# Streaming-encoder layer: more buffers in the first stage, and the recurrence's chained small products spread over more steps

## The chip, the cores and the metric

The kernel runs on one core of one Trainium2 chip. The metric is the device time of one execution in microseconds (us), as the median of three runs. A core has a matrix engine (TensorE, PE in the profile), a vector engine (VectorE, DVE), a scalar engine (ScalarE, ACT), a general engine (GpSimd, POOL) and an engine that here only issues transfers (SyncE, SP). Each takes its instructions in the order of its own queue and waits on semaphores for the others.

## The reference

One layer of a hybrid encoder on one sequence of 2048 tokens, with 16 learned tokens ahead of it (T = 2064) and a width of 1024, all in 32-bit floats:

```python
h = concat(meta_tokens, x)                       # 2064 x 1024
p = rms_norm(h, norm_mix_pre) @ w_in             # 3080 columns:
#   a: 512   RG-LRU (input and gate branch)
#   b: 1544  forgetting attention: q, k, v of 512 each, and 8 forget columns
#   c: 1024  RWKV-7: r, k, v of 256 each, and 64 + 64 + 128 low-rank columns
mix = concat(rg_lru(p.a), forgetting_attention(p.b), rwkv7(p.c))
h = h + rms_norm(mix @ w_out, norm_mix_post)
g, v = split(causal_dwconv3(rms_norm(h, norm_ffn_pre) @ w_up))   # 2 x 2816
h = h + rms_norm((gelu(g) * v) @ w_down, norm_ffn_post)

def rwkv7_step(S, r, w, k, v, kk, a):            # per token and head, S is 64 x 64
    S = S * w - (S @ kk) * (kk * a) + v * k
    return S, S @ r
```

The RG-LRU is a gated linear recurrence over time behind a convolution of four taps. The attention is causal, with a cumulated log-sigmoid of the forget columns added to the scores. RWKV-7 is a recurrence over tokens as well; its output is normalised per head and gated.

## The kernel before

Each product of 32-bit operands is made from three matmuls. `split_load` and `load_parts` turn a weight into a rounded high half (`hi`, one ACT instruction, L166) and the rest (`lo`, one DVE instruction, L167), and `mm3` (L172 to L174) adds hi·hi, hi·lo and lo·hi. The whole layer is one program of four stages: input projection with the recurrences beside it, attention, output projection, feed-forward. The change is in the first stage alone.

**The first stage** goes through the tokens in three parts of two blocks each (`w_in_tokens`): 400 and 384 tokens in part 0, 384 and 384 in part 1, 256 and 256 in part 2. `w_in_norm` loads a part's token tiles (`xt`, 128 x 1024), squares them on ACT (`xj`, L118), scales them on DVE, transposes them on PE (`pst`, L143) and splits them into `xh` and `xl`. Then come the *units* of the part, each 128 columns of w_in: first a gate unit (the forget columns, `psf`), then 8 of kind c, 4 a, 4 k, 4 v, 4 q. A unit is two blocks of 24 matmuls into a PSUM bank (`psp`); the pool `ps_mm` has five banks, which the transposes share. In part 0 a unit's weights are loaded from w_in, rounded, and stored to the DRAM scratch `wk`; parts 1 and 2 load the two halves `wh` and `wl` from there (L216). The pool `w` holds two pairs. Results leave PSUM through the pool `st`: `sth` has two buffers, `stl` (the low halves of q and k, and the gate's result `fo`) one, `stv` (turned v tiles, and the scratch `xj`) one. The pool `nt` has four buffers of 128 x 1024 with the tag `nt_x`, for token tiles, raw weights, and w_out's split.

**Beside the products** run the generators of `recurrences` through the class `Beside`, from unit 14 (`READY` + 1) of each part on: after each unit it takes `PACE` = 2 steps. A step is what stands between two `yield`s of `gate_block`, `R.block` and `lru_block`. `R.block(b)` (with `chunks`) is the RWKV recurrence of nine blocks of tokens in chunked form: it prepares the operands, solves 16 x 16 systems on DVE and POOL, and then joins them by three links of small products of 32 x 32 (`small`, L1179; PSUM tiles `rps` and `eps`). Each link needs a sum that DVE made from the one before: `u1` (L1189) from the first, `x1` (L1195) from the second, `u2` (L1209) within the third. What follows after the solved systems is kept as `R.ending` and runs in the steps of the next block, ahead of its `lru_block`. The state is `k["st"]`, copied in and out per block.

**Also in the units' loop** of parts 1 and 2 stand two side jobs: at even units a step of `up_sums` (POOL and DMA work on the feed-forward's weights, tiles `us`), at odd units of part 1 a step of `w_out_split`, which loads 128 rows of w_out, rounds them, and stores both halves (`wo`, stores at L1472), all in one step:

```python
if part and (i % 2 == 0 or part == 1 and i > 1):
    with tc.issue_after(core.loaded.ins):
        next(split_out if i % 2 else sums, None)
```

`core.loaded` is the last issued weight transfer; `issue_after` keeps what is inside it behind that instruction in the queue of the same engine, without waiting for its end.

**What sets the order.** A planner sorts the instructions of each engine by a simulated timeline; the order in which the program emits them is its input, together with the buffers of the pools. So where a yield stands decides which products an operation is emitted beside, and the planner may still move it. All DMA transfers named here are issued by SP, so its queue has an order of its own: a store there waits for what it stores, and all transfers behind it wait with it.

## Time and profile before

| | |
|---|---|
| median of three runs | 3032.07 us (3030.17 to 3035.79) |
| profiled execution | 3036.12 us, span 3034.4 us |
| mean granted TensorE clock | 0.976 |
| PE busy | 2901.2 us, 96% |
| PE weight load busy | 2484.8 us, 82% |
| DVE busy | 2042.7 us, 67% |
| ACT busy | 1481.7 us, 49% |
| POOL busy | 1305.8 us, 43% |
| hardware DMA queue of SP | 526.17 MB, 57.5% of 16 engines |

Rows of the timeline read: start in us, duration, engine, line of the kernel, operation, output <- inputs, size, and how many instructions of the same kind follow each other (x8 are eight). In brackets stands how long the engine had been idle before it and what released it, so "[1.56 <-DMA scr_ql<-stl]" is an idle time of 1.56 us that ended when the store of `stl` was done. A row of the list of waits reads: the waiting operation, what it waited for, then the total us, how often, and the longest. Rows with a stretch (such as 255.00:305.00) give length, then busy us and count for PE, its weight loads, DVE, ACT and POOL, the granted clock as a share of full speed, the DMA engines' share and GB/s. SPq is SP's issuing queue. Names: `psp` and `psf` are the projection's products, `pst` and `psv` transposes, `rps` and `eps` products of the recurrences; names in rw and lu belong to RWKV and RG-LRU, `sc` and `xu` being operands of the links; `scr_` is scratch in DRAM, `scr_qh` and `scr_ql` that of q's halves, `scr_p` that of columns a and c.

### The profile page before, as it was taken

To read this page: it belongs to the slowest core of one execution; us is meant where nothing else is said; L and a number is where in the kernel's file an instruction comes from. 1 tells how busy PE (TensorE), PEld (TensorE's weight loads), DVE (VectorE), ACT (ScalarE), POOL (GpSimd) and SP (SyncE) were. 2 spreads that over 40 slices of the span, in tenths; PEclk is the share of its full clock that TensorE was granted. 3 is DMA by queue.
4 is the path that set the end of the run, shared out by engine and by line. 5 is a ranking of instruction groups with operands and counts; after the bars stand their busy time and mean duration, and the time that the engine had idled before them with its cause. 6 is when DMAs were issued, how large, how long until landed. Compare 5 with 4: busy or idle time off the path is not lost. (4 is left out here: it accounts for less than half of the span.)

```text
span 3034.4 us, 52800 instructions
## 1 busy us (share of the span) xinstructions
PE 2901.2 (96%) x18694; PEld 2484.8 (82%) x18694; DVE 2042.7 (67%) x3947; ACT 1481.7 (49%) x2858; POOL 1305.8 (43%) x1567
## 2 busy tenths in 40 slices
PE   6998999999988999999989999999999999999998
PEld 6998898888876654566558999999999999787887
DVE  5257645666667886555627798798778777656666
ACT  4245342434336554444534566666666665424433
POOL 1001121122223665666763467545655444656443
PEclk9998999999988998999999999999999999999999
DMA  6776478566654346543426465567777774436453
GB/s 208 243 234 215 158 241 286 159 221 198 211 138 106 96 106 196 124 107 95 107 65 222 156 203 179 181 195 217 215 213 213 213 203 130 169 111 215 143 183 119
DMA packets 469189, 530.48 MB, mean 175 GB/s; under 512 B 85710, under 2 KB 355736, under 8 KB 467372
## 3 DMA queue, kind: packets, MB, share of 16 engines
q1 hardware_dynamic: 468156, 526.17, 57.5%
q8 instruction: 147, 2.41, 0.3%
q0 software_dynamic: 768, 0.93, 0.1%
q14 instruction: 118, 0.97, 0.1%
HBM read 368.07 MB, written 158.90 MB: 174 GB/s over the span
## 5 line engine op out<-in xcount | busy, mean ns | idle before, releaser
L173 PE MATMUL psu<-xo,uw 128*128 128x344 f32 x1848 | 592.6, 321 | 0.0
L172 PE MATMUL psu<-xo,uw 128*128 128x344 f32 x1848 | 587.1, 322 | 5.1 <-ACT ga L1793 3.3
L174 PE MATMUL psu<-xo,uw 128*128 128x344 f32 x1848 | 582.0, 320 | 0.0
L172 PE MATMUL psp<-xh,wh 128*128 128x384 f32 (+2 forms) x1152 | 382.0, 332 | 4.6 <-ACT wh L166 3.3
L174 PE MATMUL psp<-xh,wl 128*128 128x384 f32 (+2 forms) x1152 | 379.9, 330 | 4.2 <-DMA wl<-scr_wk 4.2
L173 PE MATMUL psp<-xl,wh 128*128 128x384 f32 (+2 forms) x1152 | 378.8, 329 | 0.0
L1622 DVE TENSOR_TENSOR uw<-uq,uw 128x512 fp32r<-128x512 f32 x341 | 323.4, 953 | 55.3 <-ACT uw L1621 52.7
L172 PEld LDWEIGHTS psu<-xo,uw 128*128 128x128 f32 x1848 | 346.8, 188 | 6.7 <-ACT ga L1793 3.6
L173 PEld LDWEIGHTS psu<-xo,uw 128*128 128x128 f32 x1848 | 348.2, 188 | 0.0
L174 PEld LDWEIGHTS psu<-xo,uw 128*128 128x128 f32 x1848 | 346.5, 188 | 0.0
L1621 ACT ACTIVATE uw<-uq 128x512 fp32r<-128x512 f32 x462 | 288.0, 627 | 89.8 <-PE psu L174 44.3
L686 ACT ACTIVATE p<-sc,bias 128x512 f32<-128x512 f32 (+4 forms) x352 | 197.1, 590 | 192.5 <-PE sc L682 161.0
L559 DVE TENSOR_REDUCE mc<-mx 128x1 f32<-128x512 f32 (+6 forms) x352 | 190.3, 565 | 109.9 <-PE mx L554 83.2
L1761 DVE SCALAR_TENSOR_TENSOR uy<-psu,ffn_cols,uy 128x342 f32<-128x342 f32 (+1 forms) x390 | 220.5, 567 | 64.4 <-ACT uy L1759 62.7
L1769 POOL TENSOR_TENSOR uy<-uy,uy 128x342 f32<-128x342 f32 (+1 forms) x132 | 146.2, 1108 | 237.5 <-ACT uw L1621 58.6
L725 POOL TENSOR_TENSOR acc<-acc,p 128x512 f32<-128x512 f32 (+3 forms) x208 | 221.1, 1065 | 55.8 <-DVE acc L725 27.1
L1622 POOL TENSOR_TENSOR uw<-uq,uw 128x512 fp32r<-128x512 f32 x121 | 179.3, 1482 | 140.2 <-ACT uw L1621 120.7
L174 PEld LDWEIGHTS psp<-xh,wl 128*128 128x128 f32 x1152 | 220.5, 192 | 14.3 <-issue 6.4
L172 PEld LDWEIGHTS psp<-xh,wh 128*128 128x128 f32 x1152 | 220.9, 192 | 11.3 <-issue 4.0
L173 PEld LDWEIGHTS psp<-xl,wh 128*128 128x128 f32 x1152 | 220.6, 192 | 7.5 <-issue 5.4
L1622 DVE TENSOR_TENSOR fo<-u,fo 128x896 fp32r<-128x896 f32 x88 | 100.4, 1140 | 130.4 <-ACT fo L1621 128.5
L1621 ACT ACTIVATE fo<-u 128x896 fp32r<-128x896 f32 x88 | 81.2, 923 | 204.3 <-PE psd L174 108.1
(483 smaller groups left out, 6390.9 us busy)
## 6 DMA issues: line engine op xcount, KB each, us to landing
uq<-scr_us SPq DMA_DIRECT2D x220, 256.0 KB
uq<-in_ffn_up_dram SPq DMA_DIRECT2D x209, 256.0 KB
wl<-scr_wk SPq DMA_DIRECT2D x48, 512.0 KB
wh<-scr_wk SPq DMA_DIRECT2D x48, 512.0 KB
u<-scr_ff SPq DMA_DIRECT2D x88, 256.0 KB
scr_ff<-uy SPq DMA_DIRECT2D x110, 171.0 KB
raw<-in_w_in_dram SPq DMA_DIRECT2D x24, 512.0 KB
scr_wk<-wh SPq DMA_DIRECT2D x24, 512.0 KB
```

What stands on the lines that cost most here:

```text
L172: nc.tensor.matmul(out, ah, bh, start=first, stop=False, skip_group_check=more)
L173: nc.tensor.matmul(out, ah, bl, start=False, stop=False, skip_group_check=more)
L174: nc.tensor.matmul(out, al, bh, start=False, stop=last, skip_group_check=more)
L559: self.reduced = nc.vector.tensor_reduce(mc[:rows, i, ci : ci + 1], ps[:rows, : e - a], axis=AX.X, op=ALU.max)
L686: last = nc.scalar.activation(p[:rows, :w], ps[:rows, :w], AF.Exp, bias=bias[:rows, j : j + 1])
L725: eng.tensor_tensor(a, ps_[0][0][:rows, c0:n] if start and i == 1 else a, p[:rows, : n - c0], op=ALU.add)
L1621: core.nc.scalar.activation(hi, src, AF.Copy)
L1622: (eng or core.nc.vector).tensor_tensor(lo, src, hi, op=ALU.subtract)
L1761: core.conved = stt(y[:, :n], src[:, i : n + i], cw[:, 44 * i + cc : 44 * i + cc + 1], y[:, :n], op0=ALU.mult, op1=ALU.add)
L1769: core.pooled = nc.gpsimd.tensor_tensor(v[:, :n], g[:, :n], v[:, :n], op=ALU.mult)
```

## The change

It has these parts:

- *Buffers.* `stl` and `stv` get two buffers each, and the gate's raw columns move into `stv`. The RG-LRU scratch `lu` gets two. The state becomes one tile of five places instead of a copy per block, and the constant `unit1` is written by two memsets where it is used. In part 2 two of every four units take their pair of weight buffers from the four of `nt_x`, so that with the pool `w` there are four pairs.
- *Steps.* `w_in_part` yields after each block instead of each unit (the loop counts a unit when its last block is done), and the gate gives two yields. `PACE` goes from 2 steps per unit to 1.25 per block, 2.5 per unit. `chunks` gets three more yields: after the first link, inside the third (once per group of 16), and before the products that use the links.
- *w_out's split.* Load, and rounding with the two stores, become two steps of their own, taken one per unit in part 1. The rounding is kept behind the last evacuation by ACT (`core.acted`), load and stores behind the last weight transfer.
- *Token tiles of part 1.* From the third on, the square is kept behind the last rounding of weights (`core.rounded`).

```diff
@@ -46,0 +47 @@ def __init__(self, tc, ctx):
+        self.turns = 0
@@ -56 +57 @@ def evac(self, out, src):
-            self.nc.scalar.activation(out, src, AF.Copy)
+            self.acted = self.nc.scalar.activation(out, src, AF.Copy)
@@ -122 +123 @@ def rstd_of(core, v, src, width, junk):
-def norm_transpose(core, pools, psum, src, rows, gain, pieces):
+def norm_transpose(core, pools, psum, src, rows, gain, pieces, after=nullcontext):
@@ -127 +128 @@ def norm_transpose(core, pools, psum, sr
-    junk = pools["st"].tile([P, D], BF16, tag="stv", name=core.n("xj"), bufs=1)
+    junk = pools["st"].tile([P, D], BF16, tag="stv", name=core.n("xj"))
@@ -129 +130,2 @@ def norm_transpose(core, pools, psum, sr
-    rs = rstd_of(core, v[:rows], xt[:rows], D, junk[:rows])
+    with after():
+        rs = rstd_of(core, v[:rows], xt[:rows], D, junk[:rows])
@@ -166 +168 @@ def load_parts(core, raws, src, hi, lo):
-    core.nc.scalar.activation(hi, raw[:], AF.Copy)
+    core.rounded = core.nc.scalar.activation(hi, raw[:], AF.Copy)
@@ -198 +200,3 @@ def w_in_norm(core, pools, psum, x, meta
-            norm_transpose(core, pools, psum, src, rows, gain, [(hi, lo, s - t0, 0, rows)])
+            late = part == 1 and (s, rows) not in blocks[0][2][:2]
+            after = (lambda: core.tc.issue_after(core.rounded.ins)) if late else nullcontext
+            norm_transpose(core, pools, psum, src, rows, gain, [(hi, lo, s - t0, 0, rows)], after)
@@ -213 +217,3 @@ def w_in_weights(core, pools, w_in, c0,
-        pair = [pools["w"].tile([P, KD, P], F32R, tag=s, name=core.n(s)) for s in ("wh", "wl")]
+        core.turns += part == 2
+        pl, tags = (pools["nt"], ("nt_x", "nt_x")) if core.turns % 4 > 1 else (pools["w"], ("wh", "wl"))
+        pair = [pl.tile([P, KD, P], F32R, tag=tag, name=core.n(s)) for s, tag in zip(("wh", "wl"), tags)]
@@ -233,2 +239,2 @@ def w_in_step(core, pools, psum, weights
-        ol = st.tile([P, 400], F32R, tag="stl", name=core.n("stl"), bufs=1)
-        nc.scalar.activation(oh[:, :n], ps[:, :n], AF.Copy, scale=sc)
+        ol = st.tile([P, 400], F32R, tag="stl", name=core.n("stl"))
+        core.acted = nc.scalar.activation(oh[:, :n], ps[:, :n], AF.Copy, scale=sc)
@@ -252 +258 @@ def turn():
-        ot = st.tile([P, 4, P], F32, tag="stv", name=core.n("stv"), bufs=1)
+        ot = st.tile([P, 4, P], F32, tag="stv", name=core.n("stv"))
@@ -276 +282 @@ def w_in_gate(core, pools, psum, w_in, b
-        raw = pools["w"].tile([P, KD, 8], F32, tag="fraw", name=core.n("fraw"), bufs=1)
+        raw = pools["st"].tile([P, KD, 8], F32, tag="stv", name=core.n("fraw"))
@@ -291 +297 @@ def w_in_gate(core, pools, psum, w_in, b
-        o = pools["st"].tile([8, 400], F32, tag="stl", name=core.n("fo"), bufs=1)
+        o = pools["st"].tile([8, 400], F32, tag="stl", name=core.n("fo"))
@@ -294 +300,2 @@ def w_in_gate(core, pools, psum, w_in, b
-    yield
+    yield False
+    yield True
@@ -314 +321 @@ def step(*args):
-        yield
+            yield block is blocks[-1]
@@ -320 +327 @@ def step(*args):
-        yield
+            yield kind == "q" and c0 == last[-1][2]
@@ -950,2 +957,2 @@ def rwkv_consts(core, pool, psum, w):
-    k["st"] = c.tile([P, 2, 64], F32, name="rstate")
-    nc.vector.memset(k["st"][:], 0.0)
+    k["st"] = c.tile([P, 5, 2, 64], F32, name="rstate")
+    nc.vector.memset(k["st"][:, 4], 0.0)
@@ -953,4 +959,0 @@ def rwkv_consts(core, pool, psum, w):
-
-    u1 = c.tile([P, 256], F32, name="unit1")
-    nc.vector.memset(u1[:], 0.0)
-    nc.vector.memset(u1[:, 0:256:17], 1.0)
@@ -961 +964 @@ def rwkv_consts(core, pool, psum, w):
-    k["unit"] = {1: u1, 2: u2}
+    k["unit"] = u2
@@ -1149 +1152,5 @@ def chunks(self, b, nch, sg, rav, bk, wc
-        nc.vector.tensor_copy(ix[:np_, : 16 * jw], k["unit"][parts][:np_, :])
+        if parts == 2:
+            nc.vector.tensor_copy(ix[:np_, : 16 * jw], k["unit"][:np_, :])
+        else:
+            nc.vector.memset(ix[:np_], 0.0)
+            nc.vector.memset(ix[:np_, 0:256:17], 1.0)
@@ -1189,0 +1197 @@ def chunks(self, b, nch, sg, rav, bk, wc
+        yield
@@ -1209,0 +1218 @@ def chunks(self, b, nch, sg, rav, bk, wc
+            yield
@@ -1222,0 +1232 @@ def chunks(self, b, nch, sg, rav, bk, wc
+        yield
@@ -1248,2 +1258,2 @@ def chunks(self, b, nch, sg, rav, bk, wc
-        st = self.t([P, nch + 1, 2, 64], "st")
-        nc.vector.tensor_copy(st[:, 0], k["st"][:])
+        st = k["st"]
+        nc.vector.tensor_copy(st[:, 0], st[:, 4])
@@ -1268 +1277,0 @@ def chunks(self, b, nch, sg, rav, bk, wc
-        nc.vector.tensor_copy(k["st"][:], st[:, nch])
@@ -1397 +1406 @@ def tl(s):
-        return R.t([P, 256], s)[:, :n]
+        return R.t([P, 256], s, bufs=2 if s == "lu" else 1)[:, :n]
@@ -1468,0 +1478,4 @@ def w_out_split(core, pool, w_out, scr):
+        raw = pool.tile([P, D], F32, tag="nt_x", name=core.n("raw"))
+        with core.tc.issue_after(core.loaded.ins):
+            core.nc.sync.dma_start(raw[:], w_out[k * P : (k + 1) * P, :])
+        yield
@@ -1470,3 +1483,6 @@ def w_out_split(core, pool, w_out, scr):
-        load_parts(core, (pool, "nt_x", None), w_out[k * P : (k + 1) * P, :], hi[:], lo[:])
-        for i, t in enumerate((hi, lo)):
-            core.nc.sync.dma_start(scr["wo"][k, i], t[:].bitcast(F32))
+        with core.tc.issue_after(core.acted.ins):
+            core.nc.scalar.activation(hi[:], raw[:], AF.Copy)
+        core.nc.vector.tensor_tensor(lo[:], raw[:], hi[:], op=ALU.subtract)
+        with core.tc.issue_after(core.loaded.ins):
+            for i, t in enumerate((hi, lo)):
+                core.nc.sync.dma_start(scr["wo"][k, i], t[:].bitcast(F32))
@@ -1996 +2012 @@ def second(self, pair, ks, weights, ahea
-PACE = 2.0
+PACE = 1.25
@@ -2110 +2126,2 @@ def spread(pl, vec, name):
-                    next(units)
+                    while not next(units):
+                        pass
@@ -2131,2 +2148,3 @@ def spread(pl, vec, name):
-                for i, _ in enumerate(units, READY + 1 if part == 0 else 1):
-                    if i == READY + 1:
+                i = READY + 1 if part == 0 else 1
+                for whole in units:
+                    if whole and i == READY + 1:
@@ -2135 +2153,5 @@ def spread(pl, vec, name):
-                    if part and (i % 2 == 0 or part == 1 and i > 1):
+                    if not whole:
+                        continue
+                    if part == 1 and i > 1:
+                        next(split_out, None)
+                    if part and i % 2 == 0:
@@ -2137 +2159,2 @@ def spread(pl, vec, name):
-                            next(split_out if i % 2 else sums, None)
+                            next(sums, None)
+                    i += 1
```

The planner makes a new order of it on every engine. ACT, POOL, SP and PE have as many instructions as before; DVE has ten fewer. From PE's instruction 6744 on, which lies behind the recurrences, the orders of all engines are the same.

*ACT at the end of part 0*, where the weights of the last two units (`wh_363`, `wh_366`) are rounded among the squares of part 1's token tiles (`xj`) and the evacuations of products (`sth`). Before:

```order
L118 ACTIVATE xj_408_3113,rs_409_3114<-xt_407_3111 128x1024
L166 ACTIVATE wh_363_2863<-raw_365_2865 128x1024
L234 ACTIVATE sth_335_2583<-psp_334_2558 128x384
L1063 ACTIVATE rwsq_270_2101<-rwe_267_2089,rwkv_om_1205 128x256 x2
L234 ACTIVATE sth_350_2707<-psp_349_2682 128x400
L118 ACTIVATE xj_413_3142,rs_414_3143<-xt_412_3140 128x1024
L166 ACTIVATE wh_366_2871<-raw_368_2873 128x1024
L234 ACTIVATE sth_353_2738<-psp_352_2713 128x384
```

After (the names' numbers are other ones; the last pair is `wh_362` and `wh_365`):

```order
L119 ACTIVATE xj_403_3097,rs_404_3098<-xt_402_3095 128x1024
L119 ACTIVATE xj_408_3126,rs_409_3127<-xt_407_3124 128x1024
L168 ACTIVATE wh_362_2858<-raw_364_2860 128x1024
L240 ACTIVATE sth_339_2636<-psp_338_2611 128x384
L240 ACTIVATE sth_350_2704<-psp_349_2679 128x400
L168 ACTIVATE wh_365_2866<-raw_367_2868 128x1024
L119 ACTIVATE xj_413_3155,rs_414_3156<-xt_412_3153 128x1024
L240 ACTIVATE sth_357_2797<-psp_356_2772 128x384
```

The last rounding stood behind the third square and now stands ahead of it; its raw weights were loaded well before in both orders.

*SP in part 1*, where the weights of two successive units (`wh_507`, then `wh_528`) and w_out's stores stand. Before:

```order
L216 DMA wh_507_3847<-scr_wk_78 128x1024
L216 DMA wl_508_3848<-scr_wk_78 128x1024
L243 DMA scr_p_65<-stp_480_3564 128x384
L165 DMA raw_527_4022<-in_w_out_dram 128x1024
L243 DMA scr_p_65<-stp_497_3681 128x384
L1472 DMA scr_wo_77<-wo_525_4020 128x1024
L1472 DMA scr_wo_77<-wo_526_4021 128x1024
L216 DMA wh_528_4028<-scr_wk_78 128x1024
L216 DMA wl_529_4029<-scr_wk_78 128x1024
```

After, with the weights of one unit (`wh_509`):

```order
L249 DMA scr_p_65<-stp_488_3610 128x384
L1488 DMA scr_wo_77<-wo_496_3748 128x1024
L1480 DMA raw_507_3852<-in_w_out_dram 128x1024
L1488 DMA scr_wo_77<-wo_497_3749 128x1024
L1668 DMA scr_us_76<-us_508_3854 512x1x256
L222 DMA wh_509_3864<-scr_wk_78 128x1024
L222 DMA wl_510_3865<-scr_wk_78 128x1024
```

The stores of a `wo` pair stood behind the load from which the pair is made (`raw_527`). Now they stand behind a load that was issued in an earlier step, and the next load stands between them.

*SP at the start of part 2*, where the weights of units 1 to 4 (unit 0 is the gate) are loaded. Before, `wh_907` is unit 1's, `wh_921` unit 2's, `wh_934` unit 3's:

```order
L216 DMA wh_907_6852<-scr_wk_78 128x1024
L216 DMA wl_922_6995<-scr_wk_78 128x1024
L236 DMA scr_qh_80<-sth_856_6442 128x384
L996 DMA rwraw_956_7262<-scr_p_65 128x2x257
L237 DMA scr_ql_81<-stl_857_6443 128x384
L1652 DMA scr_us_76<-us_920_6984 512x1x256
L293 DMA scr_f_67<-fo_891_6714 8x256
L216 DMA wh_921_6994<-scr_wk_78 128x1024
L293 DMA scr_f_67<-fo_894_6736 8x256
L243 DMA scr_p_65<-stp_910_6881 128x256
L216 DMA wh_934_7092<-scr_wk_78 128x1024
L216 DMA wl_935_7093<-scr_wk_78 128x1024
```

After, `wh_899` is unit 1's, `wh_917` unit 2's, `wh_930` unit 3's, `wh_957` unit 4's:

```order
L222 DMA wh_899_6779<-scr_wk_78 128x1024
L222 DMA wl_958_7240<-scr_wk_78 128x1024
L222 DMA wh_917_6983<-scr_wk_78 128x1024
L242 DMA scr_qh_80<-sth_858_6540 128x384
L243 DMA scr_ql_81<-stl_859_6541 128x384
L222 DMA wl_918_6984<-scr_wk_78 128x1024
L1668 DMA scr_us_76<-us_916_6973 512x1x256
L222 DMA wh_930_7081<-scr_wk_78 128x1024
L222 DMA wl_931_7082<-scr_wk_78 128x1024
L299 DMA scr_f_67<-fo_888_6705 8x256
L1662 DMA us_956_7229<-in_ffn_up_dram 128x2x128 x4
L222 DMA wh_957_7239<-scr_wk_78 128x1024
```

Unit 4 now stands here too. Through part 2 a pair's load stands about 130 products ahead of its first use on PE, where it stood about 30 ahead.

*PE at the links.* How many projection products stand on PE between a block's sum `x1` and its next group of small products (the third link), and between the start of the links and the second link, counted in the order of PE:

| recurrence block | 0 | 1 | 2 | 3 | 4 | 5 |
|---|---|---|---|---|---|---|
| third link, before | 4 | 15 | 8 | 0 | 2 | 6 |
| third link, after | 0 | 4 | 16 | 18 | 2 | 16 |
| first link, before | 12 | 18 | 22 | 26 | 18 | 26 |
| first link, after | 0 | 24 | 17 | 18 | 28 | 23 |

The queue of PE changes from products to small products 157 times before and 150 times after. Where the last projection product stands, 638 small products of `rps` and 20 of `eps` are still to come before, 650 and 18 after.

## The prediction

> **What bounds the kernel now.** I read the table of stretches first, to see where TensorE loses anything before the attention begins, then the lists of waits, then single stretches of the timeline. The columns of the table are busy us and count of each engine, the granted TensorE clock, the DMA share and GB/s.
>
> ```profile
> span 3034.4 us, 52800 instructions
> ...
> 40.00:255.00 215.00, 215.00 (x1210) 207.04 (x1209) 93.82 (x191) 85.34 (x148) 9.42 (x19) 1.00 0.70 226
> 255.00:305.00 50.00, 41.83 (x326) 37.91 (x327) 42.69 (x113) 25.42 (x47) 4.67 (x7) 0.83 0.68 237
> 305.00:640.00 335.00, 325.49 (x2741) 293.88 (x2734) 193.65 (x476) 121.44 (x231) 65.04 (x101) 0.98 0.66 212
> 640.00:895.00 255.00, 245.11 (x2589) 221.45 (x2589) 155.64 (x399) 108.18 (x223) 53.89 (x92) 0.97 0.61 189
> 895.00:1180.00 285.00, 252.21 (x2126) 164.62 (x2124) 220.09 (x581) 152.04 (x325) 146.66 (x230) 0.89 0.46 106
> ```
>
> The first stage runs to 895 us. TensorE has work in 215 of 215 us while only the products run, and in 41.83 of 50, 325.49 of 335 and 245.11 of 255 us afterwards: 27.6 us idle. The clock adds to that. A mean of 0.83 over 50 us, 0.98 over 335 and 0.97 over 255 is 8.5 + 6.7 + 7.7 = 22.9 us of work not done. All that this change can win back in the first stage is therefore about 50 us; vector engine, scalar engine and DMA have slack on average, and matter where TensorE waits for them. Why a short wait costs more than itself is seen here:
>
> ```profile
> 500.09 0.34 PE L173 MATMUL psp<-xl,wh 128*128 128x384 f32 x1
> 502.06 1.68 PE L1037 MATMUL eps<-rwwa,wa_up 64*128 64x256 f32 x4 [1.64 <-ACT ncref L436]
> ...
> 504.16 0.52 PE L172 MATMUL psp<-xh,wh 128*128 128x384 f32 x1
> 504.48 0.52 PE L173 MATMUL psp<-xl,wh 128*128 128x384 f32 x1
> ...
> 509.84 0.34 PE L173 MATMUL psp<-xl,wh 128*128 128x384 f32 x1
> 510.01 0.34 PE L174 MATMUL psp<-xh,wl 128*128 128x384 f32 x1
> ...
> 502.00:510.00 8.00, 7.94 (x25) 7.17 (x26) 3.72 (x6) 2.96 (x7) 0.92 (x1) 0.57 1.03 355
> ```
>
> After a wait of 1.64 us the products start 0.32 us apart instead of 0.17, and the clock of those 8 us is 0.57: 8 x 0.43 = 3.4 us lost on top. The Trainium skill, "TensorE: Matmul & The Clock Gate", section "HAM oscillation — how this bites in real kernels", gives the rule as no idle gaps over about 3.4 us. This trace does not agree: a gap of 1.64 us was followed by half speed. By that rule the clock terms below that follow shorter waits would be nothing, 7.7 us less gain, which is a rival further down.
>
> **Part 0's last weights.** The scalar engine rounds the last pair's weights behind the square of a token tile whose load is late, and the first product of that pair waits:
>
> ```profile
> 260.71 1.06 ACT L118 ACTIVATE xj<-xt 128x1024 bf16<-128x1024 f32 x1 [6.65 <-DMA xt<-in_x_dram]
> 261.77 1.04 ACT L166 ACTIVATE wh<-raw 128x1024 fp32r<-128x1024 f32 x1
> ...
> 262.86 0.45 PE L172 MATMUL psp<-xh,wh 128*128 128x400 f32 x1 [3.34 <-ACT wh L166]
> ...
> 263.00:268.00 5.00, 5.00 (x20) 5.00 (x21) 4.89 (x14) 0.57 (x2) 0.00 (x0) 0.66 0.90 302
> ```
>
> In the new order that rounding stands ahead of the square. Gain 3.3 us, and the clock of the next 5 us: 5 x 0.34 = 1.7. Sum **5.0**. Now the square and what follows it on the scalar engine come late instead; the products have five PSUM buffers to go on in, and the tile is wanted only at the turn to part 1, which the next rows show from 280 us on.
>
> **The turn from part 0 to part 1.** The low halves of q had one buffer, so the vector engine stood still for their stores twice, with the transposes' results behind it:
>
> ```profile
> 279.89 0.56 DVE L235 SCALAR_TENSOR_TENSOR stl<-psp,sth 128x384 fp32r<-128x384 f32 x1 [1.56 <-DMA scr_ql<-stl]
> ...
> 284.56 0.56 DVE L235 SCALAR_TENSOR_TENSOR stl<-psp,sth 128x384 fp32r<-128x384 f32 x1 [1.72 <-DMA scr_ql<-stl]
> ...
> 287.87 1.97 PE L143 MATMUL pst<-ident,xt 128*128 128x128 f32 x8 [1.77 <-DVE xl L150]
> 292.41 1.09 PE L1141 MATMUL rps<-ident,rwbk 128*128 128x128 f32 x4 [2.58 <-DVE rwbk L1135]
> ...
> 287.00:302.00 15.00, 11.07 (x107) 9.86 (x108) 14.74 (x43) 12.84 (x24) 1.43 (x2) 0.54 0.58 205
> ```
>
> With two buffers the 3.28 us of standing still go. TensorE's first wait, 1.8 us, goes with them; the second, 2.6, hangs on a vector engine that is busy 14.74 of 15 us here, so I count half, 1.3. The clock lost 15 x 0.46 = 6.9 us; half of that, 3.4, since small products and transposes still fill this place. Sum **6.5**, with 0 and 11.3 as ends.
>
> **w_out's split in part 1.** Load and rounding stood in one step, so the scalar engine waited for the load with the recurrence's results behind it:
>
> ```profile
> ACT wo L166 <- DMA raw<-in_w_out_dram: 32.2, 7, 12.8
> ...
> 482.81 1.06 ACT L166 ACTIVATE wo<-raw 128x1024 fp32r<-128x1024 f32 x1 [7.38 <-DMA raw<-in_w_out_dram]
> ...
> 484.37 0.44 PE L1320 MATMUL rps<-ident,rww 128*128 128x128 f32 x2 [1.29 <-ACT rww L1327]
> ```
>
> Of 32.2 us only 1.3 reached TensorE in a way that the trace shows. The new order rounds a whole unit after the load was issued. Gain **1.3**.
>
> **Weights of part 2.** A unit here is two blocks of 24 products at 0.12 us. Two pairs of buffers let the next load start only when the unit before last is done:
>
> ```profile
> 852.81 1.79 SPq L216 DMA_DIRECT2D wl<-scr_wk  x1
> ...
> 858.15 0.28 PE L172 MATMUL psp<-xh,wh 128*128 128x256 f32 x1
> 858.27 0.28 PE L173 MATMUL psp<-xl,wh 128*128 128x256 f32 x1
> 860.08 0.39 PE L174 MATMUL psp<-xh,wl 128*128 128x256 f32 x1 [1.53 <-DMA wl<-scr_wk]
> ...
> PE psp L174 <- DMA wl<-scr_wk: 3.4, 3, 1.5
> ...
> PE psp L172 <- DMA wh<-scr_wk: 1.3, 1, 1.3
> ...
> 864.00:875.00 11.00, 11.00 (x132) 10.29 (x130) 7.33 (x18) 4.39 (x9) 2.09 (x5) 0.53 0.41 137
> ```
>
> That load was issued at 852.81 and used at 860.08, 7.3 us later. Four pairs give it two units more, 2 x 48 x 0.12 = 11.5 us, so it is covered, and the four waits go: 4.7 us. The same 96 loads move the same bytes. The clock after the last of them lost 11 x 0.47 = 5.2 us, but another wait stands just behind it (last block below), so half: 2.6. Sum **7.3**.
>
> **The linked small products.** More boundaries, no more work. What they are for is a wait of this kind, in which the third group needs a sum that the vector engine has not yet reached:
>
> ```profile
> 567.84 1.19 PE L1179 MATMUL rps<-rwxu,rwsc 32*32 32x32 f32 x32 [2.13 <-DVE rwxu L1195]
> ...
> 675.93 1.28 PE L1179 MATMUL rps<-rwxu,rwsc 32*32 32x32 f32 x28 [1.15 <-DVE rwxu L1195]
> ...
> 862.99 2.69 PE L1179 MATMUL rps<-rwxu 32*32 32x32 f32 x96 [1.33 <-DVE rwxu L1189]
> ...
> 676.00:680.00 4.00, 4.00 (x44) 3.94 (x45) 3.39 (x8) 1.09 (x3) 1.14 (x3) 0.57 0.42 143
> ```
>
> By the counts given with the change, blocks 2 and 3 (at 568 and 676 us) get more products in between and lose 2.1 + 1.2 us and the 1.7 of the clock (4 x 0.43): 5.0. But block 0 now has nothing at two links, and block 1 has 4 products where 15 stood: three links at the mean of these two rows, 1.65, cost 5.0. The wait at 863 is the first link, which had 26 products already; I leave it. Sum **0**, between +5 and -7.
>
> **Costed at nothing.** Nine copies of the state less (0.2 us each) and two memsets instead of a copy, on the vector engine, which has slack wherever no term above names it. The number of steps per unit goes from 2 to 2.5, but the recurrence has more steps: where the products end, both orders stand in block 6, with 638 small products left before and 650 after, so the stretch 895 to 1180 is as uncovered as it was. If its waits fall otherwise there, its clock of 0.89 may move the time some us either way; that is in the range.
>
> **Sum.** 5.0 + 6.5 + 1.3 + 7.3 + 0 = 20.1 us. Every other instruction of the stage is also dealt anew to its queue, and waits that I do not see will appear; I charge one stall like the one at 502, 1.6 + 3.4 = 5.0. That leaves 15.1. The profiled execution took 3036.12 us (1.7 around the span), 0.13% above the median of 3032.07; the gain is absolute, so I take it from the median: **3017 us**.
>
> **Rivals.**
> - *The clock gives nothing back.* If half speed follows the small products themselves and not the waits, 1.7 + 3.4 + 2.6 fall out: 20.1 - 7.7 = 12.4, less a new stall without clock, 1.6: 3021 us. For it: 287 to 302 is full of small products. Against it: 504, which is nothing but products. The gap rule of the Trainium skill that is named above would come to the same time by another way.
> - *The stalls are only dealt anew.* The 50 us are spread over many places, and each delay removed lets TensorE reach its next wait earlier. Then 3028 to 3032. Against it: the waits for weights and for the rounding have nothing late behind them.
> - *Slower: SyncE's queue in part 1.* There the weights keep two pairs of buffers, and the new order puts w_out's two stores (and the next load between them) ahead of them. A store waits for its rounding, and everything behind it waits too:
>
> ```profile
> SPq L1472 <- ACT wo L166: 13.6, 5, 5.5
> ```
>
>   The longest such wait was 5.5 us, against 7.3 us from a weight load to its use. If each of the eight pairs of stores holds the weights as long as part 2's waits (4.7 / 4 = 1.2), with a clock loss of 1.7 to 3.4 (676 and 502), that is 23 to 37 us: 3017 + 23 = 3040 us. It decides from 2.6 us for each of the eight, (15.1 + 6) / 8. Against it: the rounding no longer waits for its load, so the stores should wait less.
>
> **How the numbers follow.** Forecast (3008 to 3022) 0.50, of which the low end needs most of the open halves; clock not returned 0.15; dealt anew 0.15; SyncE slower 0.20. About 0.2%, 6 us, is what a measurement can tell here. Faster: 0.50 + 0.15 = 0.65; same 0.15; slower 0.20. The range of 8 in 10 leaves out the best of the forecast and the upper half of the slow case: 3002 to 3040.
>
> **What would show it.** Right: no wait of products for wh or wl between 640 and 895, none for the rounding near 260, no vector engine waiting for the stores of q; the products end near 880. Wrong: products of part 1 waiting for weights with SyncE held by w_out's stores; longer half-speed stretches at the turn, where block 0's groups now stand side by side; or a start of attention as late as before although the products end earlier.

## The result, and the profile after

The changed kernel takes **3016.24 us** (median of nine runs, 3012.84 to 3029.70) where the kernel before, run beside it, takes 3035.79 us (nine runs, 3026.84 to 3047.01). The ratio is **0.9941, with a 95% interval of 0.9922 to 0.9959**: some 18 us less, between 12 and 24. Forecast were 15.1 us less. The median of the kernel before lay between 3030 and 3036 us from one group of runs to the next, so below each kernel is compared by its ratio to the runs beside it.

The profiled execution of the changed kernel took 3012.84 us (span 3011.1), 23.3 us less than that of before. It is the fastest of its nine executions, while the profiled one of before (3036.12) stands near the median of its nine and 5 to 6 us above the medians of the later groups (3030.11 to 3031.48). Differences between the two profiles are therefore some us too large. The table of stretches of the changed kernel, at the same times as before from 255 us on, and with one stretch more at its end, which is read further down:

```profile
255.00:305.00 50.00, 43.59 (x394) 36.22 (x392) 42.97 (x117) 32.19 (x63) 10.27 (x16) 0.84 0.64 208
305.00:640.00 335.00, 330.57 (x2728) 302.53 (x2728) 190.47 (x462) 116.89 (x225) 66.48 (x98) 0.98 0.70 230
640.00:895.00 255.00, 247.97 (x2667) 222.94 (x2668) 168.24 (x434) 105.04 (x217) 62.37 (x92) 0.94 0.60 181
895.00:1180.00 285.00, 262.40 (x2051) 168.09 (x2050) 209.45 (x556) 161.65 (x337) 151.69 (x235) 0.90 0.48 119
288.00:312.00 24.00, 21.82 (x276) 17.28 (x277) 21.06 (x63) 16.85 (x32) 9.65 (x14) 0.51 0.27 94
```

TensorE is idle for 6.4, 4.4 and 7.0 us in the three stretches from 255 to 895, where it was idle for 8.2, 9.5 and 9.9. The clock behind, 0.90, is as it was (0.89). The third row holds 22 us that lie behind the last product here, so its clock of 0.94 can't be set against the 0.97 of before. From the first to the last product the two kernels, before in the first row, compare like this:

```profile
38.50:894.00 855.50, 828.10 (x6844) 761.14 (x6843) 486.12 (x1177) 340.16 (x647) 133.01 (x219) 0.97 0.66 211
37.40:873.30 835.90, 819.19 (x6825) 755.77 (x6823) 488.73 (x1192) 339.09 (x648) 141.08 (x218) 0.97 0.67 216
```

TensorE is idle for 16.7 us of the stage where it was idle for 27.4, and by the records of the clock half speed takes 44.0 us where it took 44.4. So the 19.6 us are 10.7 us less idle time, nothing from the clock, and 8.9 us less busy time. Only 19 of 6844 instructions moved out of the stage; what else shortened the busy time was not found. The changed kernel's list of waits, 255 to 895 us:

```profile
PE rps L1186 <- DVE rwxu L1203: 6.5, 5, 2.1
PE pst L145 <- DVE xl L152: 2.2, 1, 2.2
PE rps L1186 <- ACT rwsc L1145: 1.9, 2, 1.7
PE rps L1273 <- DVE rstate L1277: 1.2, 1, 1.2
...
PE psp L176 <- DMA wl<-scr_wk: 0.2, 1, 0.2
```

Of the products' own waits only 0.2 us is left; before, the rounding and the weights cost 8.8 us (3.3, and 4.2 + 1.3). The links now head the list: L1186 is the old L1179, and L1203, the sum `x1`, the old L1195.

The last product of the first stage, which shows as a matmul of `psp` in the timeline, begins at 873.3 us, 20.7 earlier than the 894.0 of before. Nearly all of the gain is there. From it to the attention's last product of p and v pass 673.6 us, before 677.2, and what lies behind that is as long as it was (1463.2 us, now 1464.3). For each kernel of the next part this table has the same two numbers, read from its one profiled execution, with the ratio of its timed runs:

| kernel | last product of the first stage, us | from there to the attention's last product, us | ratio to before, 95% interval |
|---|---|---|---|
| before | 894.0 | 677.2 | 1 |
| changed | 873.3 | 673.6 | 0.9941 (0.9922 to 0.9959) |
| before + four pairs in part 2 | 885.5 | 669.0 | 0.9968 (0.9956 to 0.9981) |
| before + squares kept back | 890.1 | 673.4 | 0.9991 (0.9981 to 1.0002) |
| before + buffers of stl and stv | 878.1 | 680.7 | 0.9996 (0.9985 to 1.0007) |
| before + steps | 895.8 | 666.4 | 1.0023 (1.0011 to 1.0035) |
| before + w_out's own steps | 884.6 | 692.7 | 1.0065 (1.0042 to 1.0088) |
| before, 2.25 steps per unit | 892.6 | 670.8 | 0.9998 (0.9984 to 1.0013) |
| changed - steps | 885.3 | 670.2 | 0.9958 (0.9943 to 0.9972) |
| changed - w_out's own steps | 885.1 | 685.3 | 1.0024 (1.0009 to 1.0039) |
| changed - four pairs | 878.5 | 676.1 | 0.9958 (0.9942 to 0.9973) |
| changed - yields at the links | 888.0 | 665.0 | 0.9960 (0.9943 to 0.9977) |

How far one profile can be trusted is seen in the kernel with the squares kept back: from its last product on, every engine and SyncE's queue work in the order of before, and still that way takes 673.4 us against 677.2. Differences of 4 us in these two columns say nothing.

### The profile page after: what moved, and what is told of

Same layout as the page of the kernel before. It is cut to its first block, busy times and chain, and to the rows that moved or that the text cites. A ratio compares the mean times of both kernels' runs of the same rounds, so it can differ in the third digit from the quotient of the medians.

```text
span 3011.1 us, 52783 instructions
## 1 busy us (share of the span) xinstructions
PE 2901.2 (96%) x18694; PEld 2487.0 (83%) x18694; DVE 2039.1 (68%) x3937; ACT 1479.4 (49%) x2858; POOL 1314.8 (44%) x1567
## 4 chain that ended last, share of the span: by engine, by line
PE 44%; DVE 2%; DMA 1%; POOL 1%; ACT 1%; issue 1%; SPq 0%; DVEq 0%; POOLq 0%; ACTq 0%
PE psu L174 9%; PE psu L175 9%; PE psu L176 9%; PE psd L174 4%; PE psd L175 4%; PE psd L176 4%; PE pswo L174 1%; PE pswo L176 1%; PE pswo L175 1%; PE pst L1604 1%; DMA uq<-scr_us 0%; POOL dw L1638 0%; DVE uw L1638 0%; PE po L711 0%; POOL u L1903 0%
```

## The experiments

The theory was the sum of the prediction: each part takes away a wait of its own, and the links are worth nothing. The rivals were that the clock gives nothing back, that stalls are only dealt anew, and that w_out's stores hold the weights.

**Four pairs of weight buffers in part 2, alone.**

```diff
+        self.turns = 0
...
+        core.turns += part == 2
+        pl, tags = (pools["nt"], ("nt_x", "nt_x")) if core.turns % 4 > 1 else (pools["w"], ("wh", "wl"))
-        pair = [pools["w"].tile([P, KD, P], F32R, tag=s, name=core.n(s)) for s in ("wh", "wl")]
+        pair = [pl.tile([P, KD, P], F32R, tag=tag, name=core.n(s)) for s, tag in zip(("wh", "wl"), tags)]
```

> The kernel before with one thing more: in part 2 two of every four units take their weight buffers from nt_x, so four pairs. My term is 7.3 us (4.7 us of waits and 2.6 us of clock): 0.9976 of the time before, no product waiting for wh or wl after 640 us, and no half-speed stretch of 10 us at 864. If the clock gives nothing back: 4.7 us, 0.9985. If the stalls are only dealt anew, the waits for weights go and links or transposes of the recurrence wait as much more: within 2 us of before.

Measured: 0.9968, 9.7 us less (5.8 to 13.3). Of the products' waits for these loads 0.6 us is left, the 10 us of half speed at 864 us are gone, and the first stage ends 8.5 us earlier. This term was right in kind and, within the interval, in size.

**The squares of part 1 kept behind the rounding, alone.**

```diff
-    rs = rstd_of(core, v[:rows], xt[:rows], D, junk[:rows])
+    with after():
+        rs = rstd_of(core, v[:rows], xt[:rows], D, junk[:rows])
...
+            late = part == 1 and (s, rows) not in blocks[0][2][:2]
+            after = (lambda: core.tc.issue_after(core.rounded.ins)) if late else nullcontext
...
```

> The kernel before with one thing more: the squares of part 1's token tiles, from the third on, are kept behind the last rounding of weights. My term is 5.0 us: 0.9984, no product waiting for the rounding near 260 us and full clock there. Without the clock: 3.3 us, 0.9989. Dealt anew: the transposes of part 1 wait instead, since tiles that were squared early now come late; then the stretch 255 to 305 stays as idle as before, about 8 us, and the time within 2 us.

Measured: 0.9991 (0.9981 to 1.0002), 2.7 us less with no change inside the interval. The wait for `wh` is gone, with one of 1.7 us for the low half `wl` in its place, and the products end 3.9 us earlier. This is from the list of its waits (lines L166 and L167 of before are L167 and L168 here):

```profile
PE psp L175 <- DMA wl<-scr_wk: 3.5, 4, 2.1
...
PE psp L175 <- DVE wl L168: 1.7, 1, 1.7
```

**The buffers of stl and stv, alone**, with what makes room for them (the gate's columns, the state, the unit matrix):

```diff
-        ol = st.tile([P, 400], F32R, tag="stl", name=core.n("stl"), bufs=1)
+        ol = st.tile([P, 400], F32R, tag="stl", name=core.n("stl"))
...
-        ot = st.tile([P, 4, P], F32, tag="stv", name=core.n("stv"), bufs=1)
+        ot = st.tile([P, 4, P], F32, tag="stv", name=core.n("stv"))
```

> The kernel before with a second buffer for stl and stv (and the room for it: the gate's raw columns in stv, one state tile, no constant unit1). My term is 6.5 us, between 0 and 11.3: 0.9979. The vector engine must not wait for stores of q any more. The changed kernel's trace speaks against the clock half of it: its turn from part 0 to part 1 has 24 us of half speed where before had 14. If that comes from the buffers, the gain here is 0 to 3 us; if it comes from block 0's groups standing side by side, that is from the steps, the gain here is 6 us or more.

Measured: 0.9996 (0.9985 to 1.0007), no difference. The vector engine waits for no store of q, and the first stage ends 15.9 us earlier; no product waits for the rounding at 260 us either, so this part and the one above take away the same wait, and their terms do not add. But from there to the attention's end the kernel needs 680.7 us, 3.5 more than before, which two profiles of one order can differ by. The profile thus has the attention end 12.4 us earlier where the timed runs show no gain. Some 6 us of that are the slow profile of before; the rest stays open. On the alternative in the expectation the records of the clock have an answer. At the turn, between 280 and 320 us, half speed lasts 13.7 us before, 13.7 with the steps alone, 17.1 with these buffers alone, 23.9 in the changed kernel and 27.3 in the changed kernel without its steps. So the steps did not lengthen it, and none of the parts tried alone did by more than 3.4 us.

**The steps, alone.**

```diff
-        yield
+            yield block is blocks[-1]
...
+        yield
...
-PACE = 2.0
+PACE = 1.25
```

> The kernel before with the steps alone: yields per block of products, 1.25 steps per yield, three more yields in the recurrence; no buffer, no new order of w_out or of the squares. My term is 0, between 5 us less and 7 us more. The changed kernel's waits at the links (8.4 us in all, against 5.0 before) say 3 us more plus some clock: 1.001 to 1.002. If the steps carry the gain of the change by work that is better spread over the products, the time is 0.995 or so.

Measured: 1.0023 (1.0011 to 1.0035), 7 us more. The first stage ends 1.8 us later in the profile, which is the fastest of this kernel's twelve executions (7.9 us under their median) and can't show where the time went. So the steps are no gain by themselves; they cost the upper end of the range that they were given.

**w_out's load and rounding in steps of their own, alone.**

```diff
-        load_parts(core, (pool, "nt_x", None), w_out[k * P : (k + 1) * P, :], hi[:], lo[:])
+        raw = pool.tile([P, D], F32, tag="nt_x", name=core.n("raw"))
+        with core.tc.issue_after(core.loaded.ins):
+            core.nc.sync.dma_start(raw[:], w_out[k * P : (k + 1) * P, :])
+        yield
...
+        with core.tc.issue_after(core.acted.ins):
+            core.nc.scalar.activation(hi[:], raw[:], AF.Copy)
```

> The kernel before with one thing more: w_out's load and its rounding with the stores in steps of their own, one per unit of part 1. My term is 1.3 us: 0.9996, no wait of the scalar engine for w_out's load (32.2 us before). The slower rival has SyncE held by the stores, ahead of weights that have only two pairs of buffers: 23 us more, 1.0076, with waits of products for wh or wl between 305 and 631 us.

Measured: 1.0065 (1.0042 to 1.0088), 19.7 us more. That is near the time of the slower rival, but not by its mechanism. The stores wait for the rounding for 2.4 us in all, where they had waited 14.6 us (13.6 of them in the stretch of the prediction), and no product waits for a weight between 305 and 631 us. The list of SyncE, and then the products' only waits for weights, which lie behind 750 us:

```profile
SPq L1479 <- ACT wo L1475: 2.4, 5, 0.5
SPq L1479 <- DVE wo L1476: 1.2, 3, 0.5
...
PE psp L174 <- DMA wl<-scr_wk: 3.2, 2, 1.9
```

The first stage even ends 9.4 us earlier. The time is lost behind it: 692.7 us to the attention's end, 15.5 more. In the stretch in which the end of the recurrence and the start of the attention share TensorE, this kernel (first row; second row: before, from its own start of the attention) is granted less clock:

```profile
897.00:1139.00 242.00, 224.85 (x1879) 153.17 (x1879) 175.24 (x495) 133.08 (x288) 121.55 (x198) 0.83 0.41 99
```

```profile
911.00:1145.00 234.00, 213.26 (x1869) 142.85 (x1869) 186.96 (x498) 137.46 (x295) 122.85 (x202) 0.92 0.42 99
```

242 x 0.17 = 41 us of work not done against 234 x 0.08 = 19. These two stretches leave out what lies between the last product and their starts. Over the whole way behind the products the records of the clock come to 51 us against 39, so the clock makes some 12 of the 15.5 us; TensorE is idle as long as before (51.9 and 52.0 us).

**The changed kernel with its steps undone.**

```diff
-            yield block is blocks[-1]
+        yield
...
-PACE = 1.25
+PACE = 2.0
```

> The changed kernel with its steps undone: yields per unit, 2 steps per unit, no yields at the links; the buffers, the four pairs in part 2, w_out's own steps and the kept-back squares stay. If the steps are worth nothing, as in my sum, the time is that of the changed kernel, 0.994 of before, within 3 us. If the steps cost (third links wait 6.5 us against 3.3): 3 to 6 us faster than the changed kernel, 0.992 to 0.993. If they carry the gain: 0.998 to 1.0.

Measured: 0.9958 (0.9943 to 0.9972) against 0.9941. The intervals overlap, so the timed runs don't tell the two apart. In the profiles the first stage ends 12 us later without the steps, but the one profile is the fastest of nine executions and the other the slowest of five. On the kernel before, the same steps had made it 1.8 us longer.

**The changed kernel with w_out in one step again.** The diff is that of w_out's own steps, read from + to -.

> The changed kernel with w_out's load, rounding and stores in one step again, at odd units of part 1. Alone on the kernel before, the two steps cost 17 to 20 us, although the profile showed its products ending 9 us earlier: the attention behind them was 12 us longer. Theory A (the loss came from another order of the attention, which the planner deals anew with every edit): here the first stage is 1 to 4 us longer than in the changed kernel, and the whole within 10 us of it, either way. Theory B (the stores hold SyncE's queue): here the first stage is shorter than in the changed kernel, and the whole 10 to 20 us faster, 0.988 to 0.991 of before.

Measured: 1.0024 (1.0009 to 1.0039): with every other part of the change in place, the kernel is slower than the one before. Neither theory held. Theory B falls outright. Of A, the whole is 25 us slower and not within 10, the first stage is not 1 to 4 us longer but 11.8, and the way behind it is 11.7 longer as well (685.3 against 673.6). In the first stage the loss is mostly clock: half speed takes 66.3 us of it, 44.0 in the changed kernel, which costs 11.1 us. Behind it, the four computing engines have the order of the changed kernel from 1284 us on (1260 there), and both kernels take 286.3 us from there to the attention's last product, so the loss lies ahead of that. The scalar engine waits for w_out's load again:

```profile
ACT wo L168 <- DMA raw<-in_w_out_dram: 19.8, 7, 5.0
```

Behind the products, from 885 to 1580 us, the attention's scores and maxima wait longer. This is the list of TensorE's waits of this kernel:

```profile
PE sc L688 <- ACT p L693: 15.5, 18, 5.9
PE mx L561 <- DVE mc L566: 11.5, 13, 3.0
```

And the same rows of the changed kernel:

```profile
PE sc L688 <- ACT p L693: 7.3, 17, 1.0
...
PE mx L561 <- DVE mc L566: 6.5, 12, 1.9
```

The same edit thus costs 0.65% on the kernel before and is worth 0.83% (1.0024 against 0.9941) in the changed one, with intervals that lie far apart.

**The changed kernel with two pairs in part 2 again**, and **without the yields at the links**:

```diff
-        pl, tags = (pools["nt"], ("nt_x", "nt_x")) if core.turns % 4 > 1 else (pools["w"], ("wh", "wl"))
+        pl, tags = pools["w"], ("wh", "wl")
```

> The changed kernel with two pairs of weight buffers in part 2 again. My term of 7.3 us comes back in the first stage: its products end at 879 to 882 us instead of 873, with waits for wh and wl of 3 to 6 us behind 640 us. The whole: 7 us more than the changed kernel, 0.9965 of before, if the attention keeps its length of about 422 us; if the attention's order counts as much as the term, anything between 0.991 and 1.0.

```diff
...
             nc.vector.tensor_copy(u2[32:64, g], ps[32:64, :m])
-            yield
...
```

> The changed kernel without the three yields in the recurrence, the rest of its steps kept. If those yields do nothing, as in my sum, the first stage is within 2 us of the changed kernel's 836 us (first to last product) and the waits at the links are 6 to 9 us. If they cost: the waits fall to the 5 us of before, and the stage is 3 to 5 us shorter, 0.993. If they helped: waits of 10 us or more, 0.996.

Measured: 0.9958 and 0.9960, neither clear of the changed kernel's 0.9941. With two pairs, waits for `wl` of 2.5 us come back and the first stage ends 5.2 us later, of 7.3 forecast. Without the yields the links' waits are these, 10.5 us in all against 8.4 with them; the stage ends 14.7 us later, and the way behind is 8.6 us shorter. By both numbers that is the case in which the yields helped (10 us or more, 0.996), but the timed runs don't tell it from the changed kernel:

```profile
PE rps L1186 <- DVE rwxu L1202: 3.7, 4, 1.7
PE rps L1186 <- ACT rwsc L1145: 2.7, 3, 1.7
PE rps L1186 <- POOL rwitmp L1162: 2.3, 1, 2.3
...
PE rps L1186 <- ACT rwe L1042: 1.8, 1, 1.8
```

**An edit without an aim.**

```diff
-PACE = 2.0
+PACE = 2.25
```

> The kernel before with 2.25 steps per unit in place of 2, nothing else: an edit without an aim, which deals the orders anew. It shows how much such a new deal alone moves. If little, the first stage (856 us from first to last product) stays within 4 us and the whole within 3 us. If much, as the attention's lengths of 414 to 438 us in the runs so far suggest, both move by 5 to 15 us, either way.

Measured: 0.9998 (0.9984 to 1.0013). In the profile the first stage ends 1.4 us earlier and the way behind is 6.4 us shorter, of which some 5 us are the slow profile of before. The timed runs show no difference, though the recurrence's last product begins at 1122 us instead of 1146. A new deal by itself does not have to move the time.

**Waits put among products.** What follows is about the clock alone. Both kernels do extra work that is thrown away, so their times mean nothing.

```diff
+        nc.vector.tensor_copy(d[:], core.last[:, 0:P])
+        for _ in range(copies):
+            nc.vector.tensor_copy(d[:], d[:])
+        core.gate = nc.tensor.transpose(pt[:, 0:P], d[:], core.ident[:])
...
+    with core.tc.issue_after(core.gate.ins):
         for k in range(KD):
             mm3(nc, ps[:, :n], wh[:, k], wl[:, k], hi[:, k], lo[:, k], k == 0, k == KD - 1)
```

> The kernel before with six waits put into part 0, in the stretch where only products run: ahead of one block of products a transpose is added that needs the end of a chain of 2, 5, 8, 11, 14 or 18 copies on the vector engine, which starts when the block before is done. The transposed copy is not used. Theory: a wait of 1.5 to 2 us is enough to halve the granted clock afterwards, though nothing but full-size products stands on both sides; so the three or four longer waits are each followed by 3.4 us or more of half speed and the two shortest by none. Rival (the clock follows the small products themselves): no half speed in this stretch at all, whatever the wait. By the page named in the prediction, only waits over 3.4 us would do it.

Four waits fell among products only, or nearly so; the last two did not, since small products of the recurrence's preparation were drawn into them. Two were of some 4 us, and behind each the clock is half; in the longer one half speed begins 1.7 us before its end. The stretch behind the shorter second wait (1.6 us idle, 1.8 us from one matmul's start to the next) is at full clock; the first was under 1 us. Stretches of this kernel behind the waits, that of 1.8 us, of 3.8 and of 4.6:

```profile
74.00:80.00 6.00, 5.93 (x33) 5.93 (x34) 0.02 (x1) 0.50 (x1) 0.00 (x0) 1.00 0.66 203
96.70:100.10 3.40, 3.40 (x12) 3.35 (x11) 0.00 (x0) 0.00 (x0) 0.00 (x0) 0.51 0.49 144
119.00:124.00 5.00, 5.00 (x16) 4.95 (x17) 0.00 (x0) 0.00 (x0) 0.00 (x0) 0.50 0.43 120
```

So waits alone are enough, with no small product near, and for this stretch the rival falls. The theory's 1.5 to 2 us were not enough here.

> As the kernel with the six waits, with four waits now, all in units of kind c of part 0, with chains of 9, 8, 3 and 3 copies, for waits between 1 and 4 us. In the earlier one a wait of 1.8 us was not followed by half speed, those of 3.8 to 4.9 us were. Theory: the limit lies near 2 us, so that waits from 2.0 us on are followed by half speed within 3.4 us. By the page named in the prediction it lies at 3.4 us, and shorter waits are followed by none.

Two of the four waits came out longer than meant, 6.9 and 3.45 us, and half speed began within them, at 57.8 and 85.1 us. The other two came out alike to 10 ns, with full-size products on both sides. Behind one the clock is half, behind the other it is full. The rows are matmuls of the timeline, then the stretches behind them:

```profile
105.95 0.34 PE L175 MATMUL psp<-xh,wl 128*128 128x384 f32 x1
108.76 0.30 PE L238 MATMUL pstall<-ident,stall 128*128 128x128 f32 x1 [2.47 <-DVE stall L236]
...
127.45 0.34 PE L175 MATMUL psp<-xh,wl 128*128 128x384 f32 x1
130.26 0.30 PE L238 MATMUL pstall<-ident,stall 128*128 128x128 f32 x1 [2.47 <-DVE stall L236]
...
109.00:112.40 3.40, 3.40 (x12) 3.39 (x11) 0.00 (x0) 0.00 (x0) 0.00 (x0) 0.50 1.00 314
130.40:133.80 3.40, 3.40 (x20) 3.40 (x20) 0.00 (x0) 0.00 (x0) 0.00 (x0) 1.00 1.02 322
```

A wait of 2.47 us may or may not halve the clock: the theory's limit near 2 us falls, and no length of a wait alone decides here. The Trainium skill, "TensorE: Matmul & The Clock Gate", section "HAM oscillation — how this bites in real kernels", gives the rule as no idle gaps over about 3.4 us. This trace does not agree with that figure: half speed came after 2.47 us.

## Why the prediction was right, and where it was not

*The size.* Forecast 3017 us, measured 3016.24, and the gain lies where it was put: the first stage ends 20.7 us earlier in the profile, against 20.1 us of terms less 5.0 us for a new stall. That the sum came so near is in good part luck. By its own terms some 9 of the 15.1 us were to come from waits (10.7 less 1.6) and 6 from the clock (9.4 less 3.4). The profile of the stage shows 10.7 us less idle time, nothing from the clock, and 8.9 us less busy time, for which the sum has no term. In the stage, the rival in which the clock gives nothing back is nearer to what happened than the forecast, though its 3021 us, 11 us less, lies outside the measured 12 to 24.

*Part 0's last weights (5.0).* The wait is gone and the clock near 260 us is full. Alone the part gave 2.7 us, without a clear difference from nothing. That the second buffers take away the same wait was not seen.

*The turn (6.5).* This is the step that failed. The vector engine's waits for the stores of q did go, and of TensorE's waits of 1.8 and 2.6 us at this place none over 1.7 us is left. But between 270 and 320 us its waits now come to 6.5 us in seven places, where they came to 4.9 us in three. And "the clock lost 15 x 0.46 = 6.9 us; half of that" went the other way: 288 to 312 us now run at 0.51, 11.8 us of work not done. TensorE is busy for 21.82 of these 24 us, with small products and transposes. In one stretch it is not idle at all, and half speed goes on behind it:

```profile
305.68:309.10 3.42, 3.42 (x42) 3.24 (x41) 3.41 (x8) 0.93 (x3) 0.92 (x1) 0.50 0.09 29
309.10:312.51 3.41, 3.41 (x21) 2.97 (x20) 2.69 (x7) 1.86 (x4) 1.79 (x3) 0.51 0.06 15
```

There, waits cannot be what keeps the clock down. The rival in which half speed follows the small products fits this place, and was wrong in part 0, where waits alone halved the clock.

*w_out's split (1.3).* The waits of the scalar engine are gone (32.2 us before, none in the list after). The term was mis-sized and has no fixed sign: 19.7 us lost alone, some 25 us won among the other parts. The slower rival named the right part and a price near the measured one, but its wait, stores that hold the weights, appears in no trace.

*Weights of part 2 (7.3).* Right: 5.5 us of waits before, 0.2 after, 9.7 us alone.

*The links (0, between +5 and -7).* The sign of the waits was against the change, as the counts for blocks 0 and 1 said: 5.0 us in the profile of before (3.3 + 1.3 + 0.4) and 8.4 after. Blocks 0 and 1 cost 4.0 us where 5.0 were charged, and block 2 fell from 2.1 to 0.4 as forecast. But block 4, whose 2 products stayed 2, rose from 0.4 to 1.7, and block 3, which got 18 products where none stood, rose from 1.2 to 2.1:

```profile
665.64 0.29 PE L176 MATMUL psp<-xh,wl 128*128 128x256 f32 x1
668.04 1.13 PE L1186 MATMUL rps<-rwxu,rwsc 32*32 32x32 f32 x30 [2.11 <-DVE rwxu L1203]
```

The vector engine meanwhile, up to the sum `x1` in its last row:

```profile
664.63 1.42 DVE L1056 TENSOR_TENSOR_SCAN rwe<-rst,rwe 128x512 f32<-128x512 f32 x1
665.98 0.88 DVE L1448 TENSOR_TENSOR rwlr<-rwlr,rwlraw 128x256 f32<-128x256 f32 x1
666.77 0.22 DVE L1163 TENSOR_REDUCE rwix<-rwitmp 128x8 f32<-128x80 f32 x1
666.92 0.47 DVE L1419 SCALAR_TENSOR_TENSOR rwlu<-rwlraw,lru_cols,rwlu 128x256 f32<-128x256 f32 x1
667.31 0.67 DVE L1203 TENSOR_TENSOR rwxu<-rps,rwxu 32x512 f32<-32x512 f32 x1
```

At 0.12 us each, 18 products cover 2.2 us; other work of the recurrences stood ahead of the sum for longer. Counting products in the order said who would be uncovered, and not who was covered.

*The new stall (5.0).* There is one such: at 618.8 us, at the turn to part 2, transposes wait 2.2 us for the vector engine (the second row of the list above), and 3.4 us of half speed follow: 2.2 + 1.7 = 3.9 us.

*Costed at nothing: the way behind the products.* In the changed kernel it is 3.6 us shorter, which is no difference, so the omission cost nothing here. In general it is the largest unknown: over the twelve kernels it lies between 665 and 693 us. Of the two slow kernels it is the whole loss in the one and half of it in the other. The five parts measured alone add up to 0.43% slower (-0.32 - 0.09 - 0.04 + 0.23 + 0.65); the changed kernel is 0.59% faster. It also has a sixth part, the second buffer of `lu`, which has no term in the prediction and which no run tried alone or left out. TensorE's waits for `rwlu`, 1.3 us before and 1.2 to 4.7 us in the five kernels with one part alone, are gone in all five kernels that have this buffer, but also in the one with 2.25 steps, which doesn't. How much of the 1% between sum and whole is its doing stays open. A sum of terms, each read from its own wait, is therefore no account of this result, even where it meets the time. Why w_out's steps turn their sign was not settled: each kernel has one trace, and in the two slow kernels the loss takes different forms, less clock behind the products in the one, less clock in the first stage and waits of the attention's products for the vector and scalar engines in the other.

## What to carry to other kernels

Where a planner orders every engine's queue, an edit that removes a wait also deals out what follows anew: read the gain at the stage's end and again at the end of the overlapped work behind it, and time parts alone and left out before crediting one of them. The one term with a clear releaser and nothing late behind it (weights waiting for a buffer) held its size when tried alone; the terms of order, and of clock in stretches full of small products, didn't. Compare waits, clock and busy time one by one: a right sum can come from terms that are wrong. A buffer added for one wait may remove another that a second edit was meant for.

## What the runs showed of the hardware

Not expected was that two equal waits could differ in what follows. The records of the clock have two values, full and half, and in all fourteen traces every stretch between two changes is a whole number of 3.413 us long. The starts of half speed in the kernel with the two waits of 2.47 us are 57.8, 85.1 and 109.0 us: 27.3 and 23.9 us apart, which is 8 and 7 times 3.413. On this grid the wait that was followed by half speed lies in one interval (105.6 to 109.0), and the other is cut by the end of one (129.5) into 1.7 and 0.8 us.

This can be counted over all intervals of the fourteen traces, from the first products to the attention's end. Of the intervals at full speed, TensorE was busy for less than half of the time in 128, and 122 of them were followed by half speed; it was busy for 80% or more in 5205, and 40 of them were. So the share of work in fixed intervals of 3.41 us goes with the speed of the next, and of two waits of one length their place in the intervals can decide. Busy time is not the whole of it: of 386 intervals at half speed in which TensorE was busy for over 97%, 154 were followed by half speed again, as at the turn. This was read from the traces, and not tried by moving a wait.
